# Hybrid gMLP/GLA layer: sample v evacuated by ScalarE and split later, two alternating output states, first block's z prepared 3+3+2, low rank one slot later

## The chip, the cores and the metric

The kernel runs on one core of a Trainium2 chip. The time is device time of one execution in microseconds (us), lower is better. The engines work side by side, each through its own queue in order: TensorE (PE) multiplies, VectorE (DVE) and ScalarE (ACT) work on elements and empty PSUM, GpSimd (POOL) works on SBUF alone here, and SyncE (SP) issues the DMAs. An instruction waits by semaphore for the one whose data or buffer it needs, and everything queued behind it on its engine waits too.

## What is computed

One layer of an encoder, on a prompt of 512 tokens and a sample of 2048, with the same weights:

```python
h = rmsnorm(x, norm_pre)
u_a, v_a, z_a, q_b, k_b, v_b, z_b, lr_f, lr_b = split(h @ w_in)      # 1024 -> 3104 columns
out_a = spatial_gating(gelu(u_a), gelu(v_a), w_sp, b_sp, g_v_a) * silu(z_a)
g_f = log_sigmoid(lr_f @ w_gk_fwd + b_gk_fwd) / 16                    # g_b alike
o_b = gla_direction(q, k, v_b, g_f) + flip(gla_direction(flip(q), flip(k), flip(v_b), flip(g_b)))
out_b = rmsnorm(o_b, g_norm_b) * silu(z_b)
y = x + rmsnorm(concat(out_a, out_b) @ w_out, norm_post)
```

`gla_direction` is a recurrence over chunks: a state per head is multiplied by a decay and gets each chunk's k^T v added; a chunk's output is q times the state before it, plus a product inside the chunk. The second direction needs its chunks from the last to the first.

## The kernel before

The 2560 tokens are five blocks of 512: block 0 is the prompt, blocks 1 to 4 the sample. Weights and activations of the projections are split into two half-precision parts (high and low), so that one projection of 128 x 512 outputs over 1024 inputs is 24 matmuls of three products each over 8 slices.

The order is written out by hand. The work is cut into generators, and `slot()` advances all that are pending by one step, in a fixed order: small pieces of weight preparation (`tiny`), the pending projections (`mains`) oldest first, more weight preparation (`pre`), the generators in the lists `early` and `aux`, then the matmuls of the next projection (`main`), and last the small matmuls that the steps had put aside (`late`). What one step emits goes to the engines' queues in that order. Tables of numbers in the caller say in which slot which generator starts: `extra` and `gates` for a block, `pre` and `plan` for the preparation of the weights in block 0, and the list of `out_step` calls for the start of the output stage inside block 4.

A sample block takes these projections: v of the gate (pv, 4), z of the GLA (pzb, 4), v of the GLA (pvb, 4), q and k (pqk, 4, in the order 0, 2, 1, 3), then u and z of the gate (pu, pz) in turn. Their PSUM tiles share two buffers, so a projection starts when the last but one has been emptied.

- GLA v: `g_vb`. For a sample block, L490 copies PSUM to the high part on ScalarE, and L491 makes the low part on VectorE as PSUM minus the high part. The buffer is free after L491. In the same slots VectorE runs the gates of the block (`g_gates`: L598, the scan L599, L607, L609, L610) with L605 on GpSimd beside it, and ScalarE their exponentials (L614, L617, L619).
- Low rank: `g_lr` has 64 small matmuls (plr), then VectorE's copies and 16 stream transposes (L545). It starts in slot 0 of blocks 2 to 4 and in slot 3 of block 1. Slots 0 and 1 of a block also hold the rest of the block before: the last chunk's state update on VectorE (L770) and the copies of its results on ScalarE (L771, L773), and the gate's v (gelu L411, split L427 to L430).
- First block: the weights of z are prepared slice by slice, L220 the high part on ScalarE and L221 the low part on VectorE, eight slices in four steps of two. Among them stand the steps of `g_xprep`, which prepares the sample's first block: L121 sums squares, L140 scales to the high part, L142 makes the low part on VectorE and sends both off by transposing DMAs (L131). The pool of x has two buffers, and L121 writes a new one.
- Output stage: 20 tiles of 128 tokens, prompt first, each direction's chunks from the last to the first. `g_out` loads a tile, updates the state U of the second direction (L874 to L879), multiplies q with the state before (oi), adds, normalises, and transposes to OT by DMA (L912). `g_main` does the two output halves (py), 24 matmuls each, and stores y. Tiles of the sample use GpSimd for the state at mid-chunk (`um`, L874), VectorE for decay (L876) and sum (L878), which overwrites U, and ScalarE for copying `um` to where the product reads it (L879).

Of the kernel before, what the change touches and what calls it, by code (L numbers as in the profile page):

```python
# [8 lines left out]
F32 = mybir.dt.float32  # L9
# [4 lines left out]
ALU = mybir.AluOpType  # L14
# [7 lines left out]
H = 4  # L22
# [15 lines left out]
def tile_hybrid_gmlp_gla(ctx: ExitStack, tc: tile.TileContext, x_prompt, x_sample, norm_pre, w_in,  # L38
# [444 lines left out]
    def g_vb(b, i):  # L483
        ps = proj_tok(b, i, W["vb"], f"pvb{b}_{i}")
        yield
        if b > 0:
            if i == 0:
                vb[b] = bp.tile([P, 4, 2, 512], F16, name=f"vb{b}", tag="big8")
            hi = vb[b][:, i, 0, :]
            nc.scalar.activation(hi, ps, AF.Copy, scale=KS)  # L490
            nc.vector.scalar_tensor_tensor(vb[b][:, i, 1, :], ps, KS, hi, op0=ALU.mult, op1=ALU.subtract)  # L491
            return
# [139 lines left out]
    def decay_row(rows, g):  # L632
        return spread(wst, rows, g)

    def to_mid(rows, g):
        return spread(ab[:, 0], rows, g)
# [219 lines left out]
    def g_out(t):  # L856
# [9 lines left out]
        if g in (3, 4 * NB - 1):  # L866
            nc.vector.tensor_copy(U[r], kvb)
            nc.vector.memset(kvb, 0.0)
        else:
            tmp = tp.tile([P, H, P], F32, name=f"ub{g}", tag="ga")  # L870
            mid = tmp
            if b > 0:
                mid = tp.tile([P, H, P], F32, name=f"um{g}", tag="ot")
                nc.gpsimd.tensor_tensor(mid[r], U[r], to_mid(r, g), op=ALU.mult)  # L874
            if b == 0 or g != 4:
                nc.vector.tensor_tensor(tmp[r], U[r], decay_row(r, g), op=ALU.mult)  # L876
            if g not in (0, 4):
                nc.vector.tensor_tensor(U[r], tmp[r], kvb, op=ALU.add)  # L878
            nc.scalar.activation(kvb, mid[r], AF.Copy)  # L879
        yield  # L880
# [273 lines left out]
    tiny = {0: ["vb"], 1: ["vb"], 2: ["u"], 3: ["u"], 5: ["qk", "sp"], 6: ["qk", "sp"], 10: ["z"], 12: ["z"]}  # L1154
    pre = {2: [("vb", 4)], 3: [("vb", 5)], 13: [("z", 2)], 14: [("z", 2)], 15: [("z", 2)], 16: [("z", 2)]}
    plan = {1: [("u", 1)], 3: [("qk", 1)], 4: [("u", 4), ("qk", 1), ("sp", 1)], 5: [("u", 5)], 7: [("qk", 4)],
# [9 lines left out]
    for b in range(1, NB):  # L1166
        units = ([g_v(b, i) for i in range(4)] + [g_zb(b, i) for i in range(4)] + [g_vb(b, i) for i in range(4)]
                 + [g_qk(b, c) for c in (0, 2, 1, 3)] + [f(b, h) for h in range(H) for f in (g_u, g_z)])
        extra = {}
        gates = {0: [g_lr(b)], 4: [g_gates(b)]}  # L1170
        if b == 1:
# [25 lines left out]
        else:  # L1197
# [3 lines left out]
            at(14, g_npost())  # L1201
            for s, t in ((17, 0), (18, 0), (19, 0), (19, 1), (20, 0), (20, 1), (21, 1), (22, 1), (22, 0), (23, 0)):
                at(s, out_step(t))
# [53 lines left out]
```

## Time and profile before

| | us |
|---|---|
| median of three runs | 999.48 |
| lowest, highest | 998.18, 1000.11 |
| the profiled execution, its own time | 996.7 |
| its span in the trace | 995.0 |
| PE, DVE, ACT, POOL busy | 960.3, 548.8, 448.4, 267.7 |

The span is that of the recorded instructions; 1.7 us of the profiled time lie around it. Times in the rows below count from the span's start. A timeline row reads: start, length, engine, line, operation, output<-inputs, shape, number of instructions in a row, and in brackets how long the engine stood idle ahead of it and who released it. The ends of matmuls are modelled, and the next one often starts a little ahead of such an end.

### The profile page before, as it was taken

How to read it: one execution, taken by the hardware profiler on the slowest of the kernel's cores; microseconds unless marked ns; L12 is line 12 of the kernel's file. 1: busy time of each engine (PE TensorE's matmuls, PEld its weight loads, DVE VectorE, ACT ScalarE, POOL GpSimd, SP SyncE). 2: the span in 40 equal slices, each digit the busy share in tenths (PEclk: the TensorE clock that was granted, in tenths of full speed). 3: DMA queues.
4: the chain of work that ended last, by engine and by line, in shares of the span. 5: the costliest groups of instructions: out<-in, count | busy, mean ns of one | idle time of the engine just before them, and what ended most of it. 6: DMA issues, size and time to landing. Idle time of an engine off the chain costs nothing. (4 is left out here: it accounts for less than half of the span.)

```text
span 995.0 us, 14560 instructions
## 1 busy us (share of the span) xinstructions
PE 960.3 (97%) x5621; PEld 497.5 (50%) x5621; DVE 548.8 (55%) x959; ACT 448.4 (45%) x857; POOL 267.7 (27%) x308
## 2 busy tenths in 40 slices
PE   8999979999999999999999999999998999999997
PEld 7644435654455544455444555444554444444444
DVE  6765763456543545543555534475665555656553
ACT  6779633534535363344453332543444334434341
POOL 1020212312133312043311232221343333333331
PEclk9999989999999999999999999999999999999999
DMA  9721134222344221335211421211446867777763
GB/s 308 232 89 60 43 91 123 73 85 53 85 107 132 70 85 43 96 96 159 61 56 43 106 85 54 85 64 65 148 138 212 233 215 240 220 231 220 217 184 113
DMA packets 131077, 124.92 MB, mean 126 GB/s; under 512 B 80192, under 2 KB 103616, under 8 KB 128448
## 3 DMA queue, kind: packets, MB, share of 16 engines
q1 hardware_dynamic: 131008, 124.00, 42.1%
q8 instruction: 44, 0.72, 0.3%
q14 instruction: 25, 0.20, 0.1%
HBM read 69.44 MB, written 36.70 MB: 107 GB/s over the span
## 5 line engine op out<-in xcount | busy, mean ns | idle before, releaser
L385 PEld LDWEIGHTS <-hT 128*128 128x128 f16 x1344 | 130.0, 98 | 165.6 <-issue 12.2
L937 PE MATMUL py<-wo,OT 128*128 128x512 f16 (+1 forms) x960 | 208.5, 376 | 3.3 <-DMA OT<-L 2.5
L937 PEld LDWEIGHTS <-OT 128*128 128x128 f16 x984 | 95.9, 98 | 111.4 <-DMA OT<-L 4.3
L395 PE MATMUL pz<-hT,w_z 128*128 128x512 f16 x480 | 108.5, 382 | 5.7 <-ACT w_z L220 5.7
L385 PE MATMUL pvb<-w_vb,hT 128*128 128x512 f16 x480 | 105.3, 379 | 6.0 <-DVE vb L491 6.0
L395 PE MATMUL pqk<-hT,w_qk 128*128 128x512 f16 x480 | 105.3, 379 | 2.3 <-DVE QE L510 1.9
L385 PE MATMUL pzb<-w_zb,hT 128*128 128x512 f16 x480 | 106.4, 379 | 1.0 <-DVE tb L479 1.0
L395 PE MATMUL pu<-hT,w_u 128*128 128x512 f16 x480 | 106.7, 379 | 0.0
L385 PE MATMUL pv<-w_v,hT 128*128 128x512 f16 x384 | 84.8, 379 | 1.4 <-ACT vf L411 1.4
L395 PEld LDWEIGHTS <-w_qk 128*128 128x128 f16 x480 | 46.6, 98 | 58.8 <-DVE QE L510 2.3
L395 PEld LDWEIGHTS <-w_z 128*128 128x128 f16 x480 | 45.7, 98 | 60.8 <-ACT w_z L220 6.1
L395 PEld LDWEIGHTS <-w_u 128*128 128x128 f16 x480 | 46.7, 98 | 55.0
L454 POOL TENSOR_TENSOR th<-th,gu 128x512 f32<-128x512 f32 x20 | 35.6, 1779 | 131.7 <-DVE th L453 124.1
L605 POOL TENSOR_TENSOR KE<-QE 64x1024 f32<-64x1024 f32 x10 | 29.6, 2962 | 66.0 <-DVE QE L599 46.9
L878 DVE TENSOR_TENSOR U<-ub,L 64x512 f32<-64x512 f32 x16 | 11.0, 689 | 60.6 <-POOL um L874 49.4
L468 ACT ACTIVATE th<-t 128x512 f32<-128x512 f32 x20 | 12.6, 631 | 67.7 <-DVE t L467 67.6
L125 POOL TENSOR_SCALAR xms<-xms 128x1 f32<-128x1 f32 x16 | 3.4, 211 | 141.5 <-ACT xs L121 141.1
L479 DVE SCALAR_TENSOR_TENSOR tb<-tb,pzb 128x512 f32<-128x512 f32 x20 | 13.7, 686 | 48.6 <-ACT tb L478 48.5
L465 DVE SCALAR_TENSOR_TENSOR t<-sv,gv,bsp 128x512 f32<-128x512 f32 x20 | 15.0, 748 | 45.3 <-PE sv L460 38.8
L953 ACT ACTIVATE junk<-py 128x512 f16<-128x512 f32 (+1 forms) x40 | 23.6, 591 | 33.5 <-DVE y L956 32.2
L956 DVE TENSOR_TENSOR y<-py,npost 128x512 f32<-128x512 f32 (+1 forms) x40 | 27.3, 684 | 18.3 <-PE py L937 10.5
L894 ACT ACTIVATE sq<-L 128x128 f32<-128x128 f32 x80 | 23.7, 297 | 30.3 <-DVE L L890 30.3
(350 smaller groups left out, 1487.6 us busy)
## 6 DMA issues: line engine op xcount, KB each, us to landing
L<-scr SPq DMA_DIRECT2D x20, 1280.0 KB, 6.7
out_dram<-y SPq DMA_DIRECT2D x19, 512.0 KB, 7.5
x<-in_x_sample_dram SPq DMA_DIRECT2D x16, 512.0 KB, 4.1
xres<-in_x_sample_dram SPq DMA_DIRECT2D x16, 512.0 KB, 8.3
scr<-tb SPq DMA_DIRECT2D x20, 256.0 KB, 2.0
scr<-QE SPq DMA_DIRECT2D x20, 256.0 KB, 3.1
scr<-t SPq DMA_DIRECT2D x20, 256.0 KB, 2.7
scr<-S SPq DMA_DIRECT2D x20, 256.0 KB, 2.7
```

The source lines that it names most:

```text
L385: nc.tensor.matmul(ps, lhsT=hT[b][:, k, a, i * P:(i + 1) * P], rhs=w[:, k, c, :], start=(n == 0), stop=(n == 3 * KC - 1))
L395: nc.tensor.matmul(ps, lhsT=w[:, k, c, col:col + P], rhs=hT[b][:, k, a, :], start=(n == 0), stop=(n == 3 * KC - 1))
L454: nc.gpsimd.tensor_tensor(t, t, gus[b, h], op=ALU.mult)
L465: nc.vector.scalar_tensor_tensor(t3, sv, C["gv"][:, h:h + 1], C["bsp"][:, h:h + 1, :].to_broadcast([P, 4, P]), op0=ALU.mult, op1=ALU.add)
L468: nc.scalar.activation(th, t3, AF.Square, scale=AS, accum_out=sqA[:, b, h:h + 1])
L479: nc.vector.scalar_tensor_tensor(th, th, 1.0, ps, op0=ALU.add, op1=ALU.mult)
L605: nc.gpsimd.tensor_tensor(Mv[64:128, h:h + 2], Av[64:128, h:h + 2, :, ::-1], mid[64:128, h:h + 2].to_broadcast([64, 2, 4, P]), op=ALU.subt ...
L878: nc.vector.tensor_tensor(U[r], tmp[r], kvb, op=ALU.add)
L894: nc.scalar.activation(sq[:, h, :], o[:, h, :], AF.Square, accum_out=ms[:, h:h + 1])
L937: nc.tensor.matmul(bank[:, cs], lhsT=OT[:, k, a, :], rhs=wo[n][:, k, c, cs], start=(m == 0), stop=(m == 3 * KC - 1))
L953: nc.scalar.activation(junk[:, cs], pss[j][:, cs], AF.Square, accum_out=ms[:, n + j:n + j + 1])
L956: nc.vector.tensor_tensor(y[:, n * 512:(n + 1) * 512][:, cs], pss[j][:, cs], npost[n][:, cs], op=ALU.mult)
```

## The change

1. In `g_vb`, a sample block's v is copied from PSUM in full precision by ScalarE into a tile of its own (`vbf`, in the buffers that S and ob have later); one step later ScalarE makes the high part from it and GpSimd the low part.
2. In `g_out`, tiles of the sample use two states in turn, U and `Ualt`. VectorE writes decay times the old one plus the chunk into the other, and ScalarE scales the old one by the mid-chunk decay, four heads one by one, straight to where the product reads it. `um` on GpSimd goes.
3. In block 0, the slices of z are prepared 3+3+2 over slots 13 to 15 and no longer 2+2+2+2 over slots 13 to 16.
4. `g_lr` of blocks 2 to 4 starts in slot 1.
5. In block 4 the first output tile's last two steps come one slot earlier (21 and 22).

```diff
--- before.py
+++ after.py
@@ -486,9 +486,11 @@
         if b > 0:
             if i == 0:
                 vb[b] = bp.tile([P, 4, 2, 512], F16, name=f"vb{b}", tag="big8")
-            hi = vb[b][:, i, 0, :]
-            nc.scalar.activation(hi, ps, AF.Copy, scale=KS)
-            nc.vector.scalar_tensor_tensor(vb[b][:, i, 1, :], ps, KS, hi, op0=ALU.mult, op1=ALU.subtract)
+            v = tp.tile([P, 512], F32, name=f"vbf{b}_{i}", tag=("S", "ob")[i % 2])
+            nc.scalar.activation(v, ps, AF.Copy, scale=KS)
+            yield
+            nc.scalar.activation(vb[b][:, i, 0, :], v, AF.Copy)
+            nc.gpsimd.tensor_tensor(vb[b][:, i, 1, :], v, vb[b][:, i, 0, :], op=ALU.subtract)
             return
         if i == 0:
             vb[b] = bp.tile([P, 4, 512], F32, name=f"vb{b}", tag="big8")
@@ -866,17 +868,23 @@
         if g in (3, 4 * NB - 1):
             nc.vector.tensor_copy(U[r], kvb)
             nc.vector.memset(kvb, 0.0)
+            if b > 0:
+                R3["U"] = [U, tp.tile([P, H, P], F32, name="Ualt", tag="ot")]
+        elif b > 0:
+            old, new = R3["U"]
+            if g != 4:
+                tmp = tp.tile([P, H, P], F32, name=f"ub{g}", tag="ga")
+                nc.vector.tensor_tensor(tmp[r], old[r], decay_row(r, g), op=ALU.mult)
+                nc.vector.tensor_tensor(new[r], tmp[r], kvb, op=ALU.add)
+            for h in range(H):
+                nc.scalar.activation(kvb[:, h, :], old[r, h, :], AF.Copy, scale=ab[r, 0, g, h:h + 1])
+            R3["U"] = [new, old]
         else:
             tmp = tp.tile([P, H, P], F32, name=f"ub{g}", tag="ga")
-            mid = tmp
-            if b > 0:
-                mid = tp.tile([P, H, P], F32, name=f"um{g}", tag="ot")
-                nc.gpsimd.tensor_tensor(mid[r], U[r], to_mid(r, g), op=ALU.mult)
-            if b == 0 or g != 4:
-                nc.vector.tensor_tensor(tmp[r], U[r], decay_row(r, g), op=ALU.mult)
-            if g not in (0, 4):
+            nc.vector.tensor_tensor(tmp[r], U[r], decay_row(r, g), op=ALU.mult)
+            if g > 0:
                 nc.vector.tensor_tensor(U[r], tmp[r], kvb, op=ALU.add)
-            nc.scalar.activation(kvb, mid[r], AF.Copy)
+            nc.scalar.activation(kvb, tmp[r], AF.Copy)
         yield
         ps = po.tile([P, H, P], F32, name=f"oi{g}", tag="ok")
 
@@ -1152,7 +1160,7 @@
              16: [g_gla(b, 0), g_xprep(1, 3)], 18: [g_gla(b, 1)]}
     first = {0: [g_v0_stats()], 5: [g_gates(b)]}
     tiny = {0: ["vb"], 1: ["vb"], 2: ["u"], 3: ["u"], 5: ["qk", "sp"], 6: ["qk", "sp"], 10: ["z"], 12: ["z"]}
-    pre = {2: [("vb", 4)], 3: [("vb", 5)], 13: [("z", 2)], 14: [("z", 2)], 15: [("z", 2)], 16: [("z", 2)]}
+    pre = {2: [("vb", 4)], 3: [("vb", 5)], 13: [("z", 3)], 14: [("z", 3)], 15: [("z", 2)]}
     plan = {1: [("u", 1)], 3: [("qk", 1)], 4: [("u", 4), ("qk", 1), ("sp", 1)], 5: [("u", 5)], 7: [("qk", 4)],
             8: [("qk", 5), ("sp", 1)], 9: [("sp", 2), ("z", 1)]}
     for s, u in enumerate(units):
@@ -1167,7 +1175,7 @@
         units = ([g_v(b, i) for i in range(4)] + [g_zb(b, i) for i in range(4)] + [g_vb(b, i) for i in range(4)]
                  + [g_qk(b, c) for c in (0, 2, 1, 3)] + [f(b, h) for h in range(H) for f in (g_u, g_z)])
         extra = {}
-        gates = {0: [g_lr(b)], 4: [g_gates(b)]}
+        gates = {1: [g_lr(b)], 4: [g_gates(b)]}
         if b == 1:
             gates = {3: [g_lr(b)], 6: [g_gates(b)]}
 
@@ -1199,7 +1207,7 @@
                 at(s, g_wout(*piece))
             at(6, g_out_scale(0, NB - 1))
             at(14, g_npost())
-            for s, t in ((17, 0), (18, 0), (19, 0), (19, 1), (20, 0), (20, 1), (21, 1), (22, 1), (22, 0), (23, 0)):
+            for s, t in ((17, 0), (18, 0), (19, 0), (19, 1), (20, 0), (20, 1), (21, 0), (21, 1), (22, 0), (22, 1)):
                 at(s, out_step(t))
         for s, u in enumerate(units):
             if b == NB - 1 and s == 17:
```

How this moves instructions is shown at three places; the lines of the new kernel are 2 to 8 higher than those of the old one.

*GLA v.* ScalarE in block 2, from the first evacuation, before; pvb are the products in PSUM, QE and KE the gates:

```order
L490 ACTIVATE vb_3444<-pvb_0_3418 128x512
L490 ACTIVATE vb_3444<-pvb_1_3457 128x512
L614 ACTIVATE QE_3266<-KE_3267 128x2048
L490 ACTIVATE vb_3444<-pvb_2_3485 128x512
L617 ACTIVATE KE_3267<-KE_3267 128x2048
L619 ACTIVATE ab<-ab 128x2x16
L490 ACTIVATE vb_3444<-pvb_3_3516 128x512
L121 ACTIVATE xs_2_3544,xms_2_3545<-x_2_3514 128x1024
```

and now:

```order
L490 ACTIVATE vbf_0_3453<-pvb_0_3426 128x512
L492 ACTIVATE vb_3452<-vbf_0_3453 128x512
L490 ACTIVATE vbf_1_3492<-pvb_1_3465 128x512
L616 ACTIVATE QE_3274<-KE_3275 128x2048
L492 ACTIVATE vb_3452<-vbf_1_3492 128x512
L490 ACTIVATE vbf_2_3522<-pvb_2_3495 128x512
L619 ACTIVATE KE_3275<-KE_3275 128x2048
L621 ACTIVATE ab<-ab 128x2x16
L492 ACTIVATE vb_3452<-vbf_2_3522 128x512
L490 ACTIVATE vbf_3_3555<-pvb_3_3528 128x512
```

Each high part stands one step behind its evacuation, and behind the exponentials that come between. GpSimd in block 1 has, before:

```order
L125 TENSOR_SCALAR xms_1_2152<-xms_1_2152 128x1
L126 TENSOR_TENSOR xms_1_2152<-xms_1_2152,neghalf 128x1
L605 TENSOR_TENSOR KE_2107<-QE_2106 64x1024 x2
L125 TENSOR_SCALAR xms_2_2320<-xms_2_2320 128x1
L126 TENSOR_TENSOR xms_2_2320<-xms_2_2320,neghalf 128x1
```

and now:

```order
L493 TENSOR_TENSOR vb_2219<-vbf_0_2220,vb_2219 128x512
L493 TENSOR_TENSOR vb_2219<-vbf_1_2253,vb_2219 128x512
L607 TENSOR_TENSOR KE_2107<-QE_2106 64x1024 x2
L493 TENSOR_TENSOR vb_2219<-vbf_2_2284,vb_2219 128x512
L125 TENSOR_SCALAR xms_2_2326<-xms_2_2326 128x1
L126 TENSOR_TENSOR xms_2_2326<-xms_2_2326,neghalf 128x1
L493 TENSOR_TENSOR vb_2219<-vbf_3_2322,vb_2219 128x512
```

The subtractions of tiles 0 and 1 stand ahead of the two gate instructions there, that of tile 2 right behind them. In blocks 2 to 4 the first three all stand behind.

*First block's z.* ScalarE, from the first slices of z, before; xs are the parts of x, th the gate's tanh:

```order
L220 ACTIVATE w_z<-raw_z,nps_z 128x512 x2
L121 ACTIVATE xs_1_1313,xms_1_1314<-x_1_1266 128x1024
L220 ACTIVATE w_z<-raw_z,nps_z 128x512 x2
L140 ACTIVATE xs_1_1313<-x_1_1266,xms_1_1314 128x1024
L220 ACTIVATE w_z<-raw_z,nps_z 128x512 x2
L121 ACTIVATE xs_2_1390,xms_2_1391<-x_2_1352 128x1024
L220 ACTIVATE w_z<-raw_z,nps_z 128x512 x2
L140 ACTIVATE xs_2_1390<-x_2_1352,xms_2_1391 128x1024
L452 ACTIVATE th_0_1476<-pz_0_1439,ev_z 128x512
```

and now:

```order
L220 ACTIVATE w_z<-raw_z,nps_z 128x512 x3
L121 ACTIVATE xs_1_1315,xms_1_1316<-x_1_1266 128x1024
L220 ACTIVATE w_z<-raw_z,nps_z 128x512 x3
L140 ACTIVATE xs_1_1315<-x_1_1266,xms_1_1316 128x1024
L220 ACTIVATE w_z<-raw_z,nps_z 128x512 x2
L121 ACTIVATE xs_2_1394,xms_2_1395<-x_2_1356 128x1024
L140 ACTIVATE xs_2_1394<-x_2_1356,xms_2_1395 128x1024
L452 ACTIVATE th_0_1476<-pz_0_1439,ev_z 128x512
```

The last two slices moved from behind the second L121 to ahead of it.

*Output stage.* ScalarE at a tile of the sample, before; sq are the squares of the norm, junk those of the output:

```order
L894 ACTIVATE sq_7088,oms_7089<-L_6902 128x128 x4
L879 ACTIVATE L_7007<-um_7100 64x512
L953 ACTIVATE junk_1_7132,yms_7081<-py_1_7107 128x512
L905 ACTIVATE OT<-L_6902,cols 128x4x128
L906 ACTIVATE L_6902<-L_6902 128x512
```

and now:

```order
L902 ACTIVATE sq_7122,oms_7123<-L_6934 128x128 x4
L880 ACTIVATE L_7041<-Ualt,ab 64x128 x4
L961 ACTIVATE junk_1_7167,yms_7115<-py_1_7142 128x512
L913 ACTIVATE OT<-L_6934,cols 128x4x128
L914 ACTIVATE L_6934<-L_6934 128x512
```

The four scalings stand where the copy stood, and read a state and not `um`. SP's queue at the first output tile, before; work are a chunk's keys, OT the output tile:

```order
L470 DMA scr_94<-t_1_6478 512x1x128
L775 DMA scr_94<-S_6386 128x512
L776 DMA scr_94<-ob_6486 128x512
L743 DMA_TRANSPOSE work<-work 128x4x128 x2
L912 DMA_TRANSPOSE OT<-L_6204 128x4x128 x2
L470 DMA scr_94<-t_2_6631 512x1x128
```

and now:

```order
L470 DMA scr_94<-t_1_6510 512x1x128
L777 DMA scr_94<-S_6418 128x512
L778 DMA scr_94<-ob_6518 128x512
L920 DMA_TRANSPOSE OT<-L_6236 128x4x128 x2
L745 DMA_TRANSPOSE work<-work 128x4x128 x2
L470 DMA scr_94<-t_2_6665 512x1x128
```

The transposes of OT stand ahead of those of the last chunk. VectorE's stream transposes of the low rank stand, in blocks 2 to 4, behind the state update L772 and the split of v's first tile, where they stood ahead of both.

## Rows read from the trace of the kernel before

**Rows 1.** Page, part 1: busy us, share of the span, instructions.

```profile
PE 960.3 (97%) x5621; PEld 497.5 (50%) x5621; DVE 548.8 (55%) x959; ACT 448.4 (45%) x857; POOL 267.7 (27%) x308
```

**Rows 2.** PE waits: waiter <- releaser: total us, times, longest us.

```profile
PE pvb L385 <- DVE vb L491: 6.0, 3, 2.0
PE pz L395 <- ACT w_z L220: 5.7, 1, 5.7
PE oi L885 <- ACT L L879: 3.2, 14, 0.7
...
PE py L937 <- DMA OT<-L: 2.5, 3, 1.0
PE pqk L395 <- DVE QE L510: 1.9, 1, 1.9
...
PE pv L385 <- ACT vf L411: 1.4, 3, 0.5
```

**Rows 3.** Timeline of PE, block 2: start us, us, instruction, [idle <- releaser].

```profile
382.91 5.34 PE L385 MATMUL pvb<-w_vb,hT 128*128 128x512 f16 x24 [1.98 <-DVE vb L491]
388.09 4.26 PE L395 MATMUL pqk<-hT,w_qk 128*128 128x512 f16 x19
```

**Rows 4.** Timeline, block 2, VectorE, GpSimd, ScalarE.

```profile
379.08 1.89 DVE L609 COPY ab<-QE 128x16 f32<-128x16 f32 x1
...
382.18 0.68 DVE L491 SCALAR_TENSOR_TENSOR vb<-pvb,vb 128x512 f16<-128x512 f32 x1
...
376.92 4.01 POOL L605 TENSOR_TENSOR KE<-QE 64x1024 f32<-64x1024 f32 x1 [3.49 <-DVE QE L599]
...
381.16 1.91 ACT L614 ACTIVATE QE<-KE 128x2048 f32<-128x2048 f32 x1 [4.77 <-DVE ab L610]
```

**Rows 5.** Timeline of ScalarE, block 1.

```profile
247.22 1.28 ACT L614 ACT_TABLE_LOAD   x1 [3.63 <-DVE ab L610]
```

**Rows 6.** Groups of one line: ns min/median/max, first and last start us.

```profile
L430 POOL TENSOR_TENSOR va<-vf,va x20: 1153/1158/1163, 51.3 to 636.9; 128x512 f16<-128x512 f32 x20
...
L429 ACT ACTIVATE va<-vf x20: 613/629/631, 50.6 to 636.2; 128x512 f16<-128x512 f32 x20
...
L894 ACT ACTIVATE sq<-L x80: 292/293/310, 725.7 to 968.4; 128x128 f32<-128x128 f32 x80
...
L598 DVE TENSOR_TENSOR KE<-QE,KE x10: 1214/1220/2667, 98.6 to 662.3; 128x1024 f32<-128x1024 f32 x10
```

**Rows 7.** First block: PE, ScalarE, VectorE; then a stretch with PEclk ahead of DMA.

```profile
141.95 2.74 PE L395 MATMUL pz<-hT,w_z 128*128 128x512 f16 x6 [5.66 <-ACT w_z L220]
162.63 1.67 PE L395 MATMUL pz<-hT,w_z 128*128 128x512 f16 x7
...
140.13 1.06 ACT L121 ACTIVATE xs<-x 128x1024 f16<-128x1024 f32 x1 [12.75 <-DMA hT<-xs]
...
153.44 1.06 ACT L121 ACTIVATE xs<-x 128x1024 f16<-128x1024 f32 x1 [5.24 <-DMA hT<-xs]
...
156.57 0.69 DVE L453 SCALAR_TENSOR_TENSOR th<-th,pz 128x512 f32<-128x512 f32 x1 [1.51 <-ACT th L452]
...
141.90:147.40 5.50, 5.45 (x26) 3.18 (x27) 3.32 (x5) 2.93 (x4) 1.48 (x2) 0.51 0.17 54
```

**Rows 8.** Timeline of VectorE, block 2, low rank.

```profile
329.75 5.05 DVE L545 STREAM_TRANSPOSE lrtr<-lrk 32x128 f32<-32x128 f32 x16 [0.27 <-POOL lrk L538]
```

**Rows 9.** Timeline of PE, first output half.

```profile
756.01 0.61 PE L937 MATMUL py<-wo,OT 128*128 128x512 f16 x2 [1.02 <-DMA OT<-L]
757.36 2.33 PE L937 MATMUL py<-wo,OT 128*128 128x512 f16 x10 [0.75 <-DMA OT<-L]
```

**Rows 10.** Output tiles: length, PE busy, PEclk, DMA share, GB/s; then VectorE.

```profile
774.91:786.25 11.34, 11.34 (x60) 1.00 0.86 257
810.07:821.76 11.69, 11.52 (x57) 1.00 0.65 199
...
808.67 0.69 DVE L878 TENSOR_TENSOR U<-ub,L 64x512 f32<-64x512 f32 x1 [3.53 <-POOL um L874]
```

## The prediction

> **What bounds the kernel now.** The page's engine line comes first: TensorE (PE) is busy 97% of the span of 995.0 us [rows 1], and nothing in the change alters its work but the place of 3 low-rank groups. So the change can only pay where PE stands still or runs at half clock. The second view is the list of what PE waited for [rows 2]. There the reader sees six kinds of wait that the diff touches: v of the sample blocks (pvb, 3 waits, 6.0 us), the first block's z (pz, one wait of 5.7), the state product of the output stage (oi, 14 waits, 3.2), the first transposed output tile (py, OT, 3 waits, 2.5), q/k of block 1 (pqk, 1.9) and the gate's v (pv, 3 waits, 1.4).
>
> A wait costs more than its printed idle. The matmul after the wait in [rows 3] starts at 382.91 and the next group at 388.09, which is 0.16 before the modelled end 382.91 + 5.34 = 388.25. So each wait costs its idle plus 0.16. I make the sum on the profiled execution (996.7 us), which is 2.8 under the median of the runs, and scale by 999.48 / 996.7 at the end.
>
> **1. Sample's v on ScalarE and GpSimd.** The old path releases PSUM only when VectorE's L491 has subtracted. In [rows 4] L491 of tile 1 runs at 382.18, behind L610 and L609 (379.08, 1.89 us for 128x16 elements), which ended only with GpSimd's L605 (376.92 + 4.01 = 380.93). PE waits for it until 382.91. The new path releases PSUM with ScalarE's first copy. Tile 1 is then free long before, and the next release in line is that of tile 2: in the new order ScalarE takes L614, the half-precision copy of tile 1, and then tile 2's evacuation. L614 starts at 381.16 when VectorE's L610 is done. The subtraction of tile 0 is queued on GpSimd right behind L605, so it starts at 380.93 as L610 does. If it holds L610 for its 1.16 (L430) [rows 6], L614 starts at about 382.3 and with its 1.91 ends at 384.2; the copy takes 0.63 (L429) [rows 6] to 384.8, and the evacuation, priced like the copy, ends at about 385.4. PE without its wait would start tile 3 at 382.91 - 1.98 = 380.93 and, with the pitch of 5.18 in [rows 3], want the next buffer at about 386.0. The slack is 0.6. I take the whole wait as gone in blocks 2, 3 and 4: 3 x (1.98 + 0.16) = **6.4** (low end 4.3, if one block misses the slack). Removed from VectorE are 16 L491, 0.69 each as in [rows 4], 11 us in all; added are 16 half-precision copies on ScalarE (10.1 us) and 16 subtractions on GpSimd (18.5 us). Both engines are idle for most of these slots [rows 1], so this costs nothing by itself, except in block 1.
>
> **2. Block 1's q/k.** Here PE waits 1.9 [rows 2] for VectorE's L510, which waits for ScalarE's square of the product; that is queued behind L614, whose table load had waited 3.63 for L610 [rows 5]. The new order puts GpSimd's subtractions of tiles 0 and 1 ahead of L605, so they fall beside VectorE's L598 and its scan L599. The trace shows what an L598 costs where GpSimd has an L605 at the same time: up to 2.67, against a median of 1.22 [rows 6]. A scan beside GpSimd isn't in the trace. If the scan waits as L598 did, two subtractions of 1.16 eat what the missing L491 and its waits give back, L610 waits for the third one, and ends about 1.0 later. ScalarE then also has the copy of tile 3 (0.63) ahead of q/k's square, and PE's wait grows by about **1.4**. If the scan doesn't wait, L610 is done some 3.5 us earlier, L614 starts with the evacuation of tile 3, and the 1.9 + 0.16, about **2.0**, are gone. I take -1.4, since the scan reads two tiles as L598 does; the ends are -1.9 and +2.0. The Trainium skill ("SBUF — State Buffer", Who interferes with whom) says that a VectorE instruction with two SBUF inputs and a GpSimd instruction that reads SBUF exclude each other, and that whoever issues first holds the other off completely; it speaks against moving the subtraction to GpSimd. The 2.67 of L598 agrees, and no row here shows it for the scan; by the rule this term is -1.4, without it +2.0.
>
> **3. The first block's z, split 3+3+2.** ScalarE's L121 at 140.13 had stood 12.75 us behind a transfer, with the last two slices of w_z queued behind it; PE waits for these until 141.95 and then runs at a granted clock of 0.51 (the 1.2 GHz level) for 5.5 us [rows 7]. With the slices ahead of that L121, both losses go. What is late next is the x chain, which the split doesn't shorten. VectorE now has two slices more ahead of the L142 that sends this transfer off (1.4, priced like L491's 0.68), so L121 starts near 141.5. The two copies behind it, about as long on ScalarE, are gone, so z's first tanh, the next L142 and its transfer come as late as before, and the next L121 waits until 153.4 as before [rows 7]. Behind that L121 come L468, L452 and L453, and only the last frees the PSUM buffer that the fourth z product needs. It ended at 156.57 + 0.69 = 157.26 [rows 7]; L468's input is now there in time, which I put at 0.8, so about 156.45. The fourth product started at 162.63 before [rows 7]. That is **6.2** (between 4.0, if the chain comes 2.2 later, and 7.2, if PE alone decides). The two earlier splits each make ScalarE 0.65 longer ahead of the k product at 127: hidden, because the chain sets the end.
>
> **4. Low rank a slot later.** The 16 stream transposes hold VectorE for 5.05 [rows 8], ahead of the state update that ScalarE's copies and then the gelu of pv wait for. They now follow that update: 3 x (0.47 + 0.16) = **1.9**, low end 1.0, since the same 5.05 now lies ahead of the second tile's split and may cost PE a part there. Block 1 has a table of its own and stays.
>
> **5. The first output tile a slot earlier.** PE waits 1.02 and 0.75 for its transposes, which SP's queue has behind a pair for the last chunk [rows 9]. A slot earlier, which is one product of 5.2 us and what follows it, they stand ahead of that pair, whose own product comes only after the first output half. The two waits go, with 0.16 each: 2.1, and I add 0.4 of the wait for junk that follows: **2.5** (0.9 if the second tile's transposes slide, 4.0 with all of the junk wait and the third OT wait).
>
> **6. Two alternating states.** In the steady output stage a tile takes 11.69 where oi waits, and 11.34 where it doesn't [rows 10]. The wait is the end of a chain: GpSimd's L874 is queued behind the norm's power, VectorE's L878 idles 3.53 for it because it overwrites the state [rows 10], and L879 follows. After the change nothing on GpSimd is in it: decay and sum stand on VectorE with no wait of 3.53, and ScalarE scales the old state head by head. Four such small ones cost ScalarE between 4 x 0.29 = 1.2, as the squares do (L894) [rows 6], and 4 x 0.63 = 2.5, if each took as long as a whole copy (L429) [rows 6]; I take 1.4, nearer to the squares. In the tile of [rows 10] they could start once the squares ahead of them on ScalarE are through, well before L878's old start at 808.67, and PE would need them at 821.76 - 11.69 = 810.07 less the 0.35. So PE bounds the tile: 14 waits give 14 x 0.35 = 4.9, or by idle 3.2 + 14 x 0.16 = 5.4; I take **5.2**. The low end is 0.9, the first and long wait alone, if another chain keeps the period.
>
> **The sum:** 6.4 - 1.4 + 6.2 + 1.9 + 2.5 + 5.2 = 20.8. 996.7 - 20.8 = 975.9, and times 999.48 / 996.7 this is **978.6**.
>
> **The rivals.**
> - *The scan isn't held off.* Block 1 gives +2.0: 24.2 in all, 972.5, scaled **975.2**. For it: no row shows a held scan. Against it: the two tiles that it reads.
> - *The output stage keeps 11.69.* VectorE's remaining work for a tile, or the stores that free y's two buffers, sets the period. Then term 6 is 0.9: 980.2, scaled **982.9**. Against it: one stretch in this stage already ran at 11.34 with a larger DMA share, 0.86 [rows 10].
> - *The x chain eats more of z.* Term 3 is 4.0: 978.1, scaled **980.8**. For it: the fourth z product is set by a DMA landing.
> - *The change doesn't do what it says for v.* Slack 0.6 is small: if L614 starts another 2.6 later in each block, tile 2's release is as late as tile 1's was, and term 1 is zero: 982.3, scaled **985.0**.
> - *Slower:* GpSimd's 16 subtractions, each of which holds VectorE off for 1.16 on the way to a PSUM release. If every one reached PE, 18.5 would be lost, term 1 gone, and term 2 be part of it: 6.2 + 1.9 + 2.5 + 5.2 = 15.8 against 18.5, so 999.4, scaled **1002.2**. It decides from 15.8 / 16 = 0.99 us of PE time for each subtraction. Against it: pvb no longer waits on VectorE, and ScalarE, which releases it now, stood idle 4.77 ahead of L614 [rows 4].
>
> **How the numbers follow.** Forecast 0.40, unheld scan 0.24, output stage unchanged 0.11, x chain 0.11, v without gain 0.08, slower 0.03, and 0.03 that several give-backs cancel all of it. About 0.2% (2 us) is what a measurement of this kernel can tell from no change. So faster by more 0.94, within it 0.03, slower 0.03. The range runs from the unheld scan with z and the OT waits at their upper ends (975.2 - 1.0 - 1.5, about 972.5) to v without gain and 1.5 for block 1 and the low rank at their low ends (986.5); the cases outside hold about 0.1, and the tails of those inside the rest.
>
> **What would show it.** Right: no pvb wait at tile 3 in blocks 2 to 4; the z wait of 5.7 gone and the granted clock 1.00 there, with about 1 us of waits on L453 in its place; oi without waits and tiles of 11.34; no gelu wait of 0.5; the pqk wait of block 1 near 3.3, with a scan that takes or waits longer beside the subtraction (held), or no wait (not held). Wrong: a pvb wait on ScalarE's evacuation, oi waiting on ScalarE or L898, or a new half-clock stretch, which costs as much again as the work in it.

## The result: 974.63 us, 2.4% faster

The new kernel's median is 974.63 us (974.32 to 974.89 in four runs), the old one's beside it 998.88 (998.18 to 1000.11). The ratio is 0.9756, with a 95% interval of 0.9739 to 0.9773. The forecast was 978.6 with a range of 972.5 to 986.5. The profiled execution took 974.89, its span is 973.2, so 21.8 us less than the span of before; the forecast for that difference was 20.8.

PE's busy time fell from the 960.3 of [rows 1] to 953.4, with the same 5621 matmuls. The half-clock stretch of the first block is gone, which accounts for 5.5 x (1 - 0.51) = 2.7 of it; the rest is spread over many groups and wasn't followed up. First the page's engine line, then the list of PE's waits (waiter, releaser, total us, times, longest):

```profile
PE 953.4 (98%) x5621; PEld 498.1 (51%) x5621; DVE 541.3 (56%) x943; ACT 466.9 (48%) x918; POOL 275.7 (28%) x309
```

```profile
PE py L945 <- ACT junk L961: 1.4, 2, 0.8
PE pqk L395 <- DVE QE L512: 1.4, 1, 1.4
PE pzb L385 <- DVE tb L479: 1.4, 2, 1.0
...
PE pqk L395 <- DVE KE L512: 1.2, 1, 1.2
PE pz L395 <- DVE th L453: 1.1, 1, 1.1
PE oi L893 <- ACT S L773: 1.1, 1, 1.1
PE py L945 <- DMA OT<-L: 1.0, 1, 1.0
```

Of the six kinds of wait in [rows 2], those of pvb, pv, and oi on the state are gone altogether, the 5.7 of pz has become 1.1 on VectorE's L453, the 2.5 for OT are 1.0, and block 1's 1.9 for q/k are 1.4.

Where the time went is best read by laying the two traces over each other: the start of the same product in both, and how far the new one is ahead.

| product | before | after | ahead | what lies between this mark and the last |
|---|---|---|---|---|
| fourth z product, block 0 | 162.63 | 156.68 | 5.95 | z in 3+3+2 |
| third q/k product, block 1 | 255.17 | 249.28 | 5.89 | a new wait of 0.33 at block 1's pzb, then 0.4 won at q/k |
| first pzb, block 2 | 343.53 | 337.02 | 6.51 | low rank |
| first q/k product, block 2 | 388.09 | 379.42 | 8.67 | v |
| same two marks, block 3 | 486.97, 531.52 | 477.67, 520.08 | 9.30, 11.44 | low rank, v |
| same two marks, block 4 | 631.13, 675.84 | 619.07, 661.62 | 12.06, 14.22 | low rank, v |
| last prompt tile's oi | 774.91 | 759.24 | 15.67 | start of the output stage |
| last oi but one | 950.63 | 928.94 | 21.69 | tiles of the sample |

### The profile page after: what moved, and what is told of

Same layout as the page of the kernel before. It is cut to its first block, busy times and chain, and to the rows that moved or that the text cites. A ratio compares the mean times of both kernels' runs of the same rounds, so it can differ in the third digit from the quotient of the medians.

```text
span 973.2 us, 14624 instructions
## 1 busy us (share of the span) xinstructions
PE 953.4 (98%) x5621; PEld 498.1 (51%) x5621; DVE 541.3 (56%) x943; ACT 466.9 (48%) x918; POOL 275.7 (28%) x309
## 4 chain that ended last, share of the span: by engine, by line
PE 69%; DVE 9%; ACT 7%; issue 6%; DMA 6%; POOL 2%; SPq 1%; DVEq 0%; POOLq 0%; ACTq 0%
PE py L945 17%; PE pzb L385 8%; PE pvb L385 8%; PE pu L395 7%; PE pqk L395 7%; PE pz L395 7%; PE pv L385 6%; DMA out_dram<-y 2%; PE oi L893 2%; PE X L645 1%; PE sv L460 1%; DMA scr<-S 1%; PE o L765 1%; DVE QE L512 1%; PE kv L765 1%
## 5 line engine op out<-in xcount | busy, mean ns | idle before, releaser
L607 POOL TENSOR_TENSOR KE<-QE 64x1024 f32<-64x1024 f32 x10 | 32.2, 3217 | 44.0 <-DVE QE L601 24.9
L453 DVE SCALAR_TENSOR_TENSOR th<-th,pz 128x512 f32<-128x512 f32 x20 | 13.8, 688 | 49.3 <-ACT th L452 49.3
L512 DVE SCALAR_TENSOR_TENSOR QE<-pqk,cols,QE 64x512 f32<-64x512 f32 x32 | 24.0, 750 | 28.0 <-ACT sqk L505 27.7
L430 POOL TENSOR_TENSOR va<-vf,va 128x512 f16<-128x512 f32 x20 | 23.1, 1158 | 49.2 <-ACT va L429 49.1
```

Source lines behind the costliest of these rows:

```text
L430: nc.gpsimd.tensor_tensor(lo, v, hi, op=ALU.subtract)
L453: nc.vector.scalar_tensor_tensor(t, t, 1.0, pz, op0=ALU.add, op1=ALU.mult)
L512: nc.vector.scalar_tensor_tensor(o, ps[64 * hh:64 * hh + 64, :], sd, o, op0=ALU.mult, op1=ALU.mult)
L607: nc.gpsimd.tensor_tensor(Mv[64:128, h:h + 2], Av[64:128, h:h + 2, :, ::-1], mid[64:128, h:h + 2].to_broadcast([64, 2, 4, P]), op=ALU.subt ...
```

## The experiments

All kernels below are the new kernel with one thing changed, unless the text says otherwise. Their medians are set against the new kernel's 974.63. They were taken in four groups, and the old kernel, run beside each group, had medians from 998.13 to 1000.13, so differences of under about 1 us between groups say little.

### The first block's z back to 2+2+2+2

```diff
-13: [("z", 3)], 14: [("z", 3)], 15: [("z", 2)]}
+13: [("z", 2)], 14: [("z", 2)], 15: [("z", 2)], 16: [("z", 2)]}
```

> The new kernel with the first block's z prepared 2+2+2+2 again. Theory A (each part is worth the PE time that its wait took in the trace of before, and the parts add up): PE waits 5.7 us for the last slices again and the work behind it runs at half clock, so about 5.5 us more than the new kernel, 980.1. The medians fell by 24.2 us where the two traces differ by 21.8; if the half-clock stretch is longer in runs without a profile, these 2.4 belong here and it is 982.5. Rival B (later slack takes it up): under 2 us more.

979.47 us, 4.8 more. The wait and the half clock are back as in [rows 7]. The timeline of PE and a stretch behind it (length, then busy time of PE, PEld, DVE, ACT and POOL, then PEclk) show them:

```profile
142.30 2.74 PE L395 MATMUL pz<-hT,w_z 128*128 128x512 f16 x6 [5.72 <-ACT w_z L220]
```

```profile
142.20:147.70 5.50, 5.40 (x27) 3.02 (x28) 3.30 (x4) 2.98 (x6) 1.48 (x2) 0.56 0.18 57
```

The additive theory holds, 0.7 below its 5.5. The idea that this stretch also explains why the medians fell by more than the traces doesn't: it would have given 982.5.

### The preparation in 2+3+3

```diff
-13: [("z", 3)], 14: [("z", 3)], 15: [("z", 2)]}
+13: [("z", 2)], 14: [("z", 3)], 15: [("z", 3)]}
```

> The new kernel with the first block's z prepared 2+3+3. Theory A (the x chain, a transfer that sends off the second part of x and the tanh behind it, sets the start of the fourth z product): the wait of 1.15 for k at 127.9 falls to 0.5, and the wait at the fourth z product grows by as much, so no change within 0.4 us. Rival B (the preparation itself is in PE's path): 0.7 less.

974.54 us: no change. The wait for k fell from 1.15 to 0.47, as expected, and the one at the fourth z product grew from 1.12 to 1.85. That growth alone proves nothing: with the preparation left at 3+3+2, the same wait lay between 0.81 and 1.85 in the traces of this document. But the first L121 of the x chain stood at 141.56 here and at 141.44 in the new kernel, though the k product began 0.6 earlier. With the unchanged median this speaks for the x chain as what sets the start. What makes the chain's second transfer land up to 1 us later in some runs stays open. The timeline of PE:

```profile
127.28 5.35 PE L395 MATMUL pqk<-hT,w_qk 128*128 128x512 f16 x24 [0.47 <-DVE KE L512]
...
157.54 7.03 PE L395 MATMUL pz<-hT,w_z 128*128 128x512 f16 x24 [1.85 <-DVE th L453]
```

The single profiled run of this kernel took 976.45, its other four 974.4 to 974.6. What it had more is in the product behind that wait, 7.03 us for 24 matmuls where 5.34 is usual. A stretch of PE (length, busy, PEclk) says why; the granted clock is near its lower level for 3.7 us:

```profile
157.50:161.20 3.70, 3.66 (x10) 0.56 0.37 71
161.20:164.40 3.20, 3.20 (x15) 0.98 0.00 0
```

This bears on the gap between medians and traces, below.

### Sample's v back on ScalarE and VectorE, twice

```diff
-            v = tp.tile([P, 512], F32, name=f"vbf{b}_{i}", tag=("S", "ob")[i % 2])
-            nc.scalar.activation(v, ps, AF.Copy, scale=KS)
-            yield
-            nc.scalar.activation(vb[b][:, i, 0, :], v, AF.Copy)
-            nc.gpsimd.tensor_tensor(vb[b][:, i, 1, :], v, vb[b][:, i, 0, :], op=ALU.subtract)
+            hi = vb[b][:, i, 0, :]
+            nc.scalar.activation(hi, ps, AF.Copy, scale=KS)
+            nc.vector.scalar_tensor_tensor(vb[b][:, i, 1, :], ps, KS, hi, op0=ALU.mult, op1=ALU.subtract)
```

> The new kernel with v of the sample blocks evacuated and subtracted in one step by ScalarE and VectorE again. Theory A: the three waits of 2.0 us come back, 2.15 each, and block 1's wait for q/k is 0.4 longer: 6.9 more, 981.5. Rival B (VectorE's 11 us of subtractions also delay other evacuations): 9 or more, with new waits outside pvb and pqk.

982.74 us (980.8 to 984.9), 8.1 more; in the trace the three waits and block 1's longer one are 6.9, as the additive theory has it (the trace as a whole is 6.1 longer, with some other waits shorter). Two things don't fit a cost of 6.9: the median, and the spread of 4 us in a kernel whose parent lies within 0.6. So the same kernel was profiled once more:

> The new kernel with v evacuated and subtracted by ScalarE and VectorE again, once more, for a second trace: its runs lay between 980.8 and 984.9 where the new kernel's lie within 0.6 us. Theory A: what varies are the waits of pvb, through the order in which VectorE and GpSimd get their turn; a slower run shows pvb waits of over 2.0. Rival B: the waits are 2.0 again and what varies lies elsewhere or in nothing that this trace shows.

983.19 us. The pvb waits are 2.0 each in both traces, so the first half of the expectation fell: their length doesn't vary. What follows them does. Here are the first traced run (980.98 us) and the second at the same place, block 2's fourth v product:

```profile
376.86 5.34 PE L385 MATMUL pvb<-w_vb,hT 128*128 128x512 f16 x24 [1.98 <-DVE vb L491]
```

```profile
377.61 7.03 PE L385 MATMUL pvb<-w_vb,hT 128*128 128x512 f16 x24 [1.97 <-DVE vb L491]
```

A wait of 1.98, and the 24 matmuls take 5.34; a wait of 1.97, and they take 7.03. Stretches of PE behind the three waits in the second run (length, busy, PEclk):

```profile
378.00:381.60 3.60, 3.60 (x10) 0.53 0.94 217
522.10:525.70 3.60, 3.60 (x17) 1.00 0.80 173
665.80:669.40 3.60, 3.60 (x17) 1.00 0.00 0
```

The granted clock was 0.53 for 3.6 us in block 2, and 1.00 behind the equal waits of blocks 3 and 4. So a wait near 2 us sometimes costs 1.7 us more, and sometimes nothing. That, and a z wait longer by 0.8, makes 2.5; the 2.2 between the two runs is what is left after small differences the other way. The mean granted clock recorded with each of the first six runs tells the same: it falls from 0.999 in the run of 980.76 over 0.997 (982.52, 982.97) to 0.995 in that of 984.85. A loss of 0.001 is about 1 us of such a span, so the clock accounts for the spread.

### The kernel before, traced again

No edit; it is the old kernel.

> The kernel before once more, for a second trace: its runs lie between 996 and 1004. Theory A: a run near 1000 shows longer waits of pvb, or more work at half clock behind the z wait, than the first trace (6.0 us and a clock of 0.51 for 5.5 us). Rival B: both are as in the first trace.

998.35 us, 1.65 above the first profiled run of this kernel. It shows neither: the clock is 1.00 behind the pvb waits and 0.52 behind the z wait, as before. Its waits for the state in the output stage are 4.4 in all where they were 3.2; the longest is 0.92 where it was 0.17:

```profile
846.42 1.16 PE L885 MATMUL oi<-L 128*128 128x128 f32 x8 [0.92 <-ACT L L879]
```

So for the old kernel itself no half-clock stretch behind pvb was caught in a trace. But the clock is recorded for its other runs too. The six above 1001.3 had a mean granted clock of 0.990 to 0.992, and the 32 below it 0.992 to 0.995, all but one at least 0.993. So lost clock is behind the slowest of its runs, which spread from 996 to 1004. In which places it was lost isn't recorded.

### One state again

```diff
-            old, new = R3["U"]
...
-            for h in range(H):
-                nc.scalar.activation(kvb[:, h, :], old[r, h, :], AF.Copy, scale=ab[r, 0, g, h:h + 1])
+                mid = tp.tile([P, H, P], F32, name=f"um{g}", tag="ot")
+                nc.gpsimd.tensor_tensor(mid[r], U[r], to_mid(r, g), op=ALU.mult)
...
+            nc.scalar.activation(kvb, mid[r], AF.Copy)
```

> The new kernel with one state, overwritten by VectorE, and the mid-chunk state made on GpSimd and copied by ScalarE. Theory A: tiles of 11.69 us in place of 11.25, 14 times 0.44, so 6 us more, 980.7. Rival B (the state's chain only cost its first long wait): 0.9 more.

982.36 us, 7.7 more. The waits for the state are back in 14 tiles, 4.8 us in all, and the tiles take 11.68:

```profile
PE oi L887 <- ACT L L881: 4.8, 14, 1.2
PE oi L887 <- ACT S L773: 0.8, 1, 0.8
```

```profile
841.93 1.16 PE L887 MATMUL oi<-L 128*128 128x128 f32 x8 [0.17 <-ACT L L881]
...
853.61 1.16 PE L887 MATMUL oi<-L 128*128 128x128 f32 x8 [0.16 <-ACT L L881]
```

The additive theory holds; what came beyond its 6 lies at single tiles, with waits of 1.23, 0.98 and 0.81.

### Two states, with the mid-chunk state on GpSimd

```diff
-            for h in range(H):
-                nc.scalar.activation(kvb[:, h, :], old[r, h, :], AF.Copy, scale=ab[r, 0, g, h:h + 1])
+            mid = tp.tile([P, H, P], F32, name=f"um{g}", tag="S")
+            nc.gpsimd.tensor_tensor(mid[r], old[r], to_mid(r, g), op=ALU.mult)
+            nc.scalar.activation(kvb, mid[r], AF.Copy)
```

> The new kernel with its two alternating states, but the mid-chunk state made by GpSimd in one instruction and copied by ScalarE, as before the change. Theory A: the period of 11.69 came from VectorE's sum waiting to overwrite the state that GpSimd still reads; with two states that wait goes, the product's input is ready about 0.7 earlier, and tiles take 11.25: within 0.5 us of the new kernel. Rival B: GpSimd's place behind the norm sets the period by itself, so 4 to 6 us more.

976.14 us, 1.5 more and not within 0.5, but far from the 4 to 6 of the rival. The trace puts 0.5 on the z wait of the first block, which varies by as much from run to run, and 0.8 on the first tile of the sample and one near the end. Two short waits for the state are left (0.40 and 0.26), and from the fourth tile on most tiles take what that from 805.88 to 817.13 takes, 11.25:

```profile
794.53 1.16 PE L894 MATMUL oi<-L 128*128 128x128 f32 x8 [0.26 <-ACT L L881]
...
805.88 1.05 PE L894 MATMUL oi<-L 128*128 128x128 f32 x8
...
817.13 1.05 PE L894 MATMUL oi<-L 128*128 128x128 f32 x8
```

So it is the second state that gives the period, not ScalarE's scaling. GpSimd may stay in the chain behind the norm; what had to go is VectorE's sum, which waited for GpSimd to read the state that it would overwrite, and stood ahead of ScalarE's copy.

### The subtraction in block 1

Three runs ask what GpSimd's subtractions cost in block 1, whose scans had grown in the new kernel. VectorE and GpSimd there, in the new kernel:

```profile
227.43 3.13 DVE L601 TENSOR_TENSOR_SCAN QE<-smask,KE 128x1024 f32<-128x1024 f16 x1
...
232.62 3.89 DVE L601 TENSOR_TENSOR_SCAN QE<-smask,KE 128x1024 f32<-128x1024 f16 x1
...
240.55 0.18 DVE L612 TENSOR_TENSOR ab<-QE 128x16 f32<-128x16 f32 x1
```

```profile
226.73 4.78 POOL L493 TENSOR_TENSOR vb<-vbf,vb 128x512 f16<-128x512 f32 x2 [12.11 <-ACT vb L492]
231.59 2.78 POOL L607 TENSOR_TENSOR KE<-QE 64x1024 f32<-64x1024 f32 x1
```

The first scan takes 3.13, beside a subtraction, and the second 3.89, beside the gate instruction L607 (231.59, 2.78 us); both took 2.29 before. The two subtractions take 4.78 where two alone take 2.3. Yet L612 isn't late. The first run gives the subtraction to VectorE there:

```diff
-            nc.gpsimd.tensor_tensor(vb[b][:, i, 1, :], v, vb[b][:, i, 0, :], op=ALU.subtract)
+            (nc.vector if b == 1 else nc.gpsimd).tensor_tensor(vb[b][:, i, 1, :], v, vb[b][:, i, 0, :], op=ALU.subtract)
```

> The new kernel, but in block 1 alone the low part of v is subtracted by VectorE from the copy and not by GpSimd. Theory A (GpSimd's subtractions hold VectorE's scans off: 3.13 and 3.89 us in the new trace against 2.29 before): both scans take 2.29 again, L612 ends 2 us earlier in its block, ScalarE's L616 follows, and PE's wait of 1.43 for q/k goes: 1.5 less, 973.1. Rival B (the scan is longer for another reason, or ScalarE's own queue sets the wait): scans stay long or the wait stays over 1.

974.74 us, no change. The scans are 2.29 again. But the wait for q/k stayed, at 1.55, since the second L600 (the old L598) now takes 2.94 beside the gate instruction, where it takes 1.22 alone, and VectorE does the subtractions itself:

```profile
228.22 2.29 DVE L601 TENSOR_TENSOR_SCAN QE<-smask,KE 128x1024 f32<-128x1024 f16 x1
...
231.01 2.94 DVE L600 TENSOR_TENSOR KE<-QE,KE 128x1024 f32<-128x1024 f32 x1
233.98 2.29 DVE L601 TENSOR_TENSOR_SCAN QE<-smask,KE 128x1024 f32<-128x1024 f16 x1
...
240.31 0.18 DVE L612 TENSOR_TENSOR ab<-QE 128x16 f32<-128x16 f32 x1
```

The reading that fits both: between the log (226.2) and L612 all instructions of the two engines that read two SBUF tiles go one after the other, whichever engine they are on. Without any subtraction their lengths alone are, for L600, the scan, L607, L609 and L612, 2 x 1.22 + 2 x 2.29 + 2 x 1.91 + 2.28 + 0.18 = 13.3. GpSimd's two subtractions of 1.16 make it 15.6, VectorE's two of 0.68 make it 14.7. The second run tests it, by moving the subtractions behind the stretch:

```diff
+            tags = ("S", "ob", "gm", "ga") if b == 1 else ("S", "ob", "S", "ob")
-            v = tp.tile([P, 512], F32, name=f"vbf{b}_{i}", tag=("S", "ob")[i % 2])
+            v = tp.tile([P, 512], F32, name=f"vbf{b}_{i}", tag=tags[i])
...
+            if b == 1:
+                for _ in range(4 - i):
+                    yield
             nc.gpsimd.tensor_tensor(vb[b][:, i, 1, :], v, vb[b][:, i, 0, :], op=ALU.subtract)
```

> The new kernel, but in block 1 GpSimd's four subtractions come some steps later, behind both halves of its gate instruction (four copies of v are kept in buffers of their own there). Theory A: from the log's end to L612, VectorE's and GpSimd's instructions exclude each other, so the stretch is as long as their own lengths added up, whichever engine does the subtraction; that is why moving it to VectorE left the wait at 1.55. Taken out of the stretch, the two subtractions give 2 x 1.16 = 2.3: L612 ends 2 us earlier, the scans take 2.29, and PE's wait of 1.43 goes, 1.6 less than the new kernel. Rival B: GpSimd's gate instruction on the second half sets the end whatever comes ahead of it, and the wait stays over 1.

974.05 us, no clear change, and the wait stayed at 1.40. But the stretch shrank: from 226.26 to 239.08 it is 12.8 us, against 14.6 in the new kernel (226.17 to 240.73) and 14.1 with VectorE's subtractions (226.35 to 240.49). Each is 0.5 to 1.0 below its sum, and 1.8 of the 2.3 were won. One part of the expectation failed: only the first scan takes 2.29 again. The second takes 3.88 with no subtraction near it, so what holds it is the gate instruction, and its 3.89 in the new kernel wasn't the subtractions' doing.

```profile
226.26 1.23 DVE L604 TENSOR_TENSOR KE<-QE,KE 128x1024 f32<-128x1024 f32 x1 [2.42 <-ACT QE L599]
...
230.97 3.88 DVE L605 TENSOR_TENSOR_SCAN QE<-smask,KE 128x1024 f32<-128x1024 f16 x1
...
238.90 0.18 DVE L616 TENSOR_TENSOR ab<-QE 128x16 f32<-128x16 f32 x1
```

```profile
239.15 1.28 ACT L620 ACT_TABLE_LOAD   x1 [0.93 <-DVE ab L616]
...
245.53 0.60 ACT L509 ACTIVATE sqk<-pqk 128x512 f32<-128x512 f32 x1 [1.61 <-POOL vb L497]
```

ScalarE's table load follows 1.7 earlier, and then the square of q/k waits 1.61 for GpSimd: it writes the buffer "S", in which the first tile's copy still stands unread. That is a fault of the experiment, and the third run differs from it only in that buffer:

```diff
-            tags = ("S", "ob", "gm", "ga") if b == 1 else ("S", "ob", "S", "ob")
+            tags = ("gs", "ob", "gm", "ga") if b == 1 else ("S", "ob", "S", "ob")
```

> As the run with deferred subtractions in block 1, but the copy of v's first tile isn't in the buffer that the square of q/k writes, where that run lost what it had won (the square stood 1.61 us behind GpSimd's first subtraction). Theory A: L612's counterpart ends about 1.6 earlier than in the new kernel, the table load and all behind it follow, and PE's wait of 1.43 for q/k goes: 1.5 less than the new kernel, 973.1. Rival B: ScalarE's own queue (evacuation of tile 3, table load, square of x) holds the wait over 1.

973.30 us (972.1 to 973.8, all below the new kernel's lowest), 1.3 less, and the wait for q/k is gone from the list. So the lengths of the two engines add up, but for the 0.5 to 1.0 by which they overlap, and this version is faster than both kernels: 0.9736 of the old one, with an interval of 0.9723 to 0.9749.

### Low rank back to slot 0

```diff
-        gates = {1: [g_lr(b)], 4: [g_gates(b)]}
+        gates = {0: [g_lr(b)], 4: [g_gates(b)]}
```

> The new kernel with the low rank of blocks 2 to 4 in slot 0 again. Theory A: pv waits 0.47 for the gelu three times, 0.63 each from start to start, 1.9 more than the new kernel, 976.5. Rival B: with the projections of v freed, the gelu has slack and it is under 0.7 more.

976.45 us, 1.8 more: pv waits three times again (2.4 in all in the traced run, which at 977.88 was the slowest; one wait is 1.4 there, and why wasn't followed up).

```profile
PE pv L385 <- ACT vf L411: 2.4, 3, 1.4
```

### The first output tile back by a slot

```diff
-..., (20, 1), (21, 0), (21, 1), (22, 0), (22, 1)):
+..., (20, 1), (21, 1), (22, 1), (22, 0), (23, 0)):
```

> The new kernel with the first output tile's last two steps one slot later again. Theory A: the waits of 1.02 and 0.75 for its transposes come back and what the earlier steps cost elsewhere (0.4 at the state product, 0.24 at the next tile) goes: 1.5 more, 976.1. Rival B: the transposes were hidden once the rest ran faster, no change.

976.79 us, 2.2 more; there are three waits for OT again, 2.7 in all, where the new kernel has one of 1.0.

```profile
PE py L945 <- DMA OT<-L: 2.7, 3, 1.0
PE py L945 <- ACT junk L961: 0.9, 1, 0.9
```

### The parts together

| undone | median | more than the new kernel |
|---|---|---|
| z in 3+3+2 | 979.47 | 4.8 |
| v | 982.74 | 8.1 |
| low rank | 976.45 | 1.8 |
| start of the output | 976.79 | 2.2 |
| two states | 982.36 | 7.7 |
| sum | | 24.6 |

The sum is 24.6, and the whole change gave 998.88 - 974.63 = 24.25. Within the 1 us to which medians of different groups can be compared, the parts share nothing.

## Why the prediction was right, step by step

**Sample's v: right in size, with a wrong margin.** The forecast was 6.4; the table of marks gives 2.16 + 2.14 + 2.16 = 6.46. The worry was that GpSimd's first subtraction would hold L610 (now L612) and leave a slack of 0.6. It didn't: L612 came first and the subtraction behind it. (In the old order VectorE's L142, 1.27 at 380.99, also stood between L610 and L491, which the forecast didn't name; ScalarE's release doesn't depend on it.) VectorE, GpSimd and ScalarE in block 2 of the new kernel:

```profile
373.94 0.18 DVE L612 TENSOR_TENSOR ab<-QE 128x16 f32<-128x16 f32 x1
```

```profile
374.06 1.16 POOL L493 TENSOR_TENSOR vb<-vbf,vb 128x512 f16<-128x512 f32 x1
```

```profile
376.55 0.58 ACT L490 ACTIVATE vbf<-pvb 128x512 f32<-128x512 f32 x1
```

The third tile's evacuation ends at 376.55 + 0.58 = 377.13 and PE's next product starts at 379.42, so the slack was 2.3. What the forecast had not seen is the clock: undoing this part costs 8.1 in the median, and its slower runs have the lower granted clock, since a 2.0 us wait is at times followed by half clock.

**Block 1's q/k: the scan was held, but the sign of the term was wrong.** The scan was held off, as forecast (3.13 against 2.29). The step that failed is "L610 waits for the third one, and ends about 1.0 later", where the third one is GpSimd's third subtraction. L612 (the old L610) came at 240.55, ahead of that subtraction at 240.68, and the table load that it releases came 247.22 - 242.79 = 4.4 after the start of the first q/k product before [rows 5], and 240.81 - 237.33 = 3.5 after it now. So it came 0.9 earlier: what the held scans cost was less than what VectorE won, which had idled 2.97 and 1.03 there ahead of two L491. About half of that went to tile 3's copy (L492, 0.61), which stands ahead of the square, as forecast. The wait shrank from 1.85 to 1.43: 0.4 won instead of 1.4 lost. The rule of the Trainium skill ("SBUF — State Buffer", Who interferes with whom), by which the two engines exclude each other when VectorE has two SBUF inputs and GpSimd reads SBUF, is what these runs show for the scan: 2.29 with the subtraction on VectorE, 3.13 beside GpSimd's subtraction and 3.89 beside its gate instruction. The rival with an unheld scan gave 975.2, closer to the measured time, for the wrong reason.

**The first block's z: right.** The forecast had L121 at 141.5 and 153.4, and the fourth z product at 156.45; they came at 141.44, 153.43 and 156.68.

```profile
141.44 1.06 ACT L121 ACTIVATE xs<-x 128x1024 f16<-128x1024 f32 x1 [12.69 <-DMA hT<-xs]
...
153.43 1.06 ACT L121 ACTIVATE xs<-x 128x1024 f16<-128x1024 f32 x1 [7.19 <-DMA hT<-xs]
```

```profile
156.68 3.61 PE L395 MATMUL pz<-hT,w_z 128*128 128x512 f16 x16 [1.12 <-DVE th L453]
```

That is 5.95 for 6.2. Another 0.5 went at block 1's pzb, which now waits 0.33 there (pzb waits twice, 1.4 in all, in the list above). The granted clock was 1.00 throughout, and the wait on L453 was 1.1 where about 1 was forecast.

**Low rank: right.** 0.62 + 0.63 + 0.62 = 1.9.

**Start of the output: too large.** 2.5 was forecast; the marks show 15.67 - 14.22 = 1.45, and undoing it costs 2.2. The two waits for the first tile's transposes went (2.1). But the wait for junk, which was to lose 0.4, is 0.84 still. The third wait for OT, the one left in the list, grew from 0.69 to 1.03. And the second tile's oi waits 1.1 for ScalarE where it was 0.7; with the steps back in their slots it was 0.8. So the earlier steps cost a part of what they gain, before that oi.

**Two states: right in kind, too small.** 5.2 was forecast, and 6.0 came. The term mis-sized is the period without a wait. It was taken from the one stretch of before that showed none, 11.34 [rows 10]. That is the last prompt tile, and it takes 11.33 in the new kernel too (759.24 to 770.57), so it was no measure of a sample tile that runs free. The new tiles of the sample are 11.25, in which PE is never idle (length, PE busy, PEclk, DMA share, GB/s):

```profile
793.93:805.18 11.25, 11.25 (x57) 1.00 0.64 187
816.43:827.68 11.25, 11.25 (x57) 1.00 1.00 316
```

So a tile gains 0.44 and not 0.35. The four scalings take ScalarE 1.26 together, where 1.4 was taken.

**From the profile to the median: the largest miss.** The sum for the trace was 1.0 too small (20.8 for 21.8), and that it came so close is in part luck: block 1 came out 1.8 better than forecast and the two states 0.8, the first block's z 0.7 worse with pzb's new wait, and the start of the output 1.0 worse. Of the other 3.0 between forecast and result, 2.7 come from the last step, in which 975.9 was scaled by 999.48 / 996.7. That treats the 2.8 between the median and the profiled run as something that any kernel has. The new one hasn't: its median (974.63) is 0.3 below its profiled run (974.89). The first profiled run of the old kernel had a mean granted clock of 0.996 and most of its other runs 0.993 to 0.995, so 1 to 3 us of a run are clock that this trace didn't lose. The new kernel's runs are at 0.998 and 0.999. That the old kernel lost this clock behind its pvb waits is likely, from the run with v undone; no trace of the old kernel itself shows it.

## What to carry to other kernels

Waits that a change removes on PE add up well, if each is followed to what is late next: five parts, 24.6 apart and 24.25 together. Before moving an elementwise instruction with two SBUF inputs from VectorE to GpSimd, add the lengths on both engines over the stretch in which they run side by side: the choice of engine changes the sum only by the difference of the two lengths (14.6 and 14.1 us here, with the same wait of PE), and moving it out of the stretch helps (12.8). And where a kernel's runs spread by more than those of its variants, look for waits on PE just long enough to cost clock at times, before scaling a traced sum to the median.

## What the runs showed of the hardware

- Equal waits of PE, 1.97 and 1.98 us at the same place, were followed by a granted clock of 0.53 for 3.6 us in one run and by full clock in the other. One of 1.85 was followed by 0.56 for 3.7 us in a profiled run of a kernel whose other runs were 2 us faster. Each cost 1.7 us. It is rare in the traces here: of 12 waits of 1.97 to 2.00 ahead of a v product one was followed by half clock, and of 9 waits of 1.74 to 1.86 ahead of a z or q/k product also one. Waits of 5.7 were followed by half clock in all three traces that have them.
- VectorE's scan with two SBUF inputs took 2.29 alone and up to 3.89 beside a subtraction or gate instruction on GpSimd, and GpSimd's subtraction 1.16 alone and up to 3.0 beside VectorE. Taken together the two engines needed 12.8 us for instructions whose own lengths add up to 13.3, 14.1 for 14.7 and 14.6 for 15.6, so they overlapped by 0.5 to 1.0.
- Four scalings of 64x128 by a scale from memory took ScalarE 1.26 us in a row, or 0.38 each with an overlap, where one copy of 64x512 took 0.63 (L879 before).
